# Linear ReLU attention on one core: loads in five runs of two octets and one of one, in place of two of three, two of two and one of one

## The chip, the core and the metric

The kernel runs on one core of a Trainium2 chip. The core has a matrix engine (PE, with its weight loads shown as PEld), a vector engine (DVE), a scalar engine (ACT), a general engine (POOL) and a synchronising engine (SP), and sixteen transfer (DMA) engines that are shared by all queues of the core. The metric is the time of one execution on the device in microseconds; the number compared is the median over several executions.

## The reference

```
Q, K, V: (8, 12, 512, 64) float32
Q_feat = maximum(0, Q)
K_feat = maximum(0, K)
KV          = einsum('bhkd,bhkv->bhdv', K_feat, V)
K_sum       = sum(K_feat, axis=2)
numerator   = einsum('bhqd,bhdv->bhqv', Q_feat, KV)
denominator = einsum('bhqd,bhd->bhq', Q_feat, K_sum)
return numerator / (denominator[..., None] + 1e-10)
```

There are 96 independent heads (8 x 12), each of 512 rows of 64 values. 37.75 MB are read and 12.58 MB are written.

## The kernel before

**Tiling.** Eight heads make an octet; there are `NO` = 12 octets, numbered 0 to 11. Of each input an octet is 128 partitions x 2048 values: 1 MB of float32 in memory, and 512 KB of bfloat16 once loaded, because the loads from POOL's queue convert while they copy. Octet 0 is special: its K and V are loaded unconverted by SP's and ACT's queues into `k8` and `v8`, and only its Q comes over POOL's queue.

**Rings.** K, V and Q of octets 1 to 11 go to the rings `k_all`, `v_all` and `q_all` with `RING` = 6 places; octet o lies at place (o - 1) mod 6. So octets 1 to 6 can be loaded at once, and octet 7 needs the place of octet 1.

**Runs.** `RUNS` lists how many neighbouring octets one load carries. For each run `load_octets(o, n)` issues three transfers on POOL's queue, in the order K, V, Q: `load_kv(Kr, ...)` and `load_kv(Vr, ...)` at line 106 and `load_q` at line 114 (line 111 when the run has one octet). A transfer's consumers wait until the whole transfer has landed, so the first octet of a run is not usable before the last one of that run.

**The plan.** POOL's transfers are issued in the fixed order of the list `plan`. It holds the loads of `RUNS` and, between and behind them, the stores of octets 0 to 9 (line 149); the stores of octets 10 and 11 are issued by SP (line 279). `pump(done)` runs through the plan after each octet. It issues a load once the places it overwrites have been read, and a store once its result is ready; nothing overtakes the head of the list:

```
last = o + n - 1 - RING
while done < last - HEAD + 1:          # HEAD = 4
    plan.append(("store", done, done))
...
if kind == "load" and o + n - 1 - RING <= done:
```

With the runs before, POOL's order is: Q of octet 0; octets 1 to 3; octets 4 to 6; octets 7 and 8; store 0; octets 9 and 10; store 1; octet 11; stores 2 to 9. Everything up to octet 6 is issued by the first call, `pump(0)`.

**Slots.** In the program as built, POOL's transfers take eight completion semaphores in turn. A transfer that is eight places behind another in POOL's order is issued only after that other one has landed, and POOL stands still for it.

**The octet loop.** For octet o, in program order: `kvs(o)` sums K-features times V over all rows on PE (line 196) and ACT copies the sums out of PSUM (line 205); `prep(2o+2)` masks the first half of K (DVE line 180) and V (DVE line 182) of octet o + 1, and `prep_v` does the other V mask (ACT line 187); `backs(o-1)` transposes the previous octet's result back (PE line 265), and DVE multiplies by the reciprocal denominator into `o_sb` (line 271), which is then stored; `denom(o)` (PE line 247; DVE lines 250, 255, 259); `out_t(o)` (PE line 237, ACT line 239); `prep(2o+3)` for the second half (DVE lines 180, 182, 189); `qt(o+1)` transposes Q of octet o + 1 (PE line 215, ACT line 220); `pump(o+1)`. So K and V of octet o + 1 are first needed early in the pass of octet o, and its Q at the end of that pass. Every engine takes its instructions in this order.

**Result tiles.** `o_sb` has seven buffers, two of which first hold `k8` and `v8`. The result of octet 9 goes to the buffer of octet 2, and so waits for store 2 to land.

Of the kernel before, what the change touches and what calls it, by code (L numbers as in the profile page):

```python
# [10 lines left out]
def kernel(  # L11
# [73 lines left out]
    q_sb, k_sb, v_sb = {}, {}, {}  # L85

    RING = DELAY + 1
    RUNS = (3, 3, 2, 2, 1)
    k_all = consts.tile([P, RING, RQ, D], bf16, name="k_all")
    v_all = consts.tile([P, RING, RQ, D], bf16, name="v_all")  # L90
    q_all = consts.tile([P, RING + 1, U, 2 * D], bf16, name="q_all")
# [38 lines left out]
    plan, o, done = [], 1, 0  # L130
    for n in RUNS:
        last = o + n - 1 - RING
# [231 lines left out]
```

## Time and profile before

| | |
|---|---|
| time, median of 3 | 127.46 us (126.89 to 127.71) |
| profiled execution, its own time | 128.06 us |
| its span in the profile | 126.1 us |
| mean granted PE clock | 0.91 |
| PE, DVE, ACT busy | 67%, 63%, 64% of the span |
| POOL's transfer queue (q0) | 28.31 MB in SBUF bytes, 90.2% of sixteen engines' span |

The span is what the profiler covers; the time around it (start and end of the execution) is the difference of 1.96 us. Busy shares are means over the whole span, and the first third of this kernel looks quite different from the rest. DMA rates are counted in SBUF bytes: a converting load reads twice what it writes, so it shows about half the rate of a store. All landing times below are an issue's start plus its time to landing.

### The profile page before, as it was taken

Reading aid. Unit: us, or ns where it says so; the run is one execution under the profiler, and the core shown is the slowest. Engines: PE = TensorE matmul, PEld = TensorE weight load, DVE = VectorE, ACT = ScalarE, POOL = GpSimd, SP = SyncE. Lnnn points to the kernel's source line nnn. Section 1 sums busy time; section 2 is a strip of 40 time slices with the busy share of each in tenths; the row PEclk is TensorE's granted clock in tenths of the full one; section 3 lists DMA queues with packets and bytes.
Section 4 is the critical chain, followed back from the end, with each engine's and each line's share of the span. In section 5 each row is a group of like instructions: output and inputs, shape, how many; then the busy total and the mean of one; then the engine's idle time right before and its main releaser. Section 6 shows DMA issues by size and latency. Waiting matters only on the chain.

```text
span 126.1 us, 3357 instructions
## 1 busy us (share of the span) xinstructions
PE 84.3 (67%) x1451; PEld 75.3 (60%) x1451; DVE 79.6 (63%) x175; ACT 80.4 (64%) x110; POOL 17.7 (14%) x32
## 2 busy tenths in 40 slices
PE   0005951000399898988989898998989899898600
PEld 0005940000399687878978787897878788796500
DVE  2709530067003979969696987969697896928510
ACT  0008840063065989899898989989898998975000
POOL 6920000000000070002604110110220010100000
PEclk9999985555558999999999999999999999999996
DMA  3999999999999999999999999999999999999762
GB/s 81 387 318 213 218 212 217 214 213 216 216 213 213 221 209 214 220 209 216 216 213 231 365 213 210 216 216 326 265 216 304 411 431 421 421 421 416 301 249 94
DMA packets 6638, 32.71 MB, mean 259 GB/s; under 512 B 480, under 2 KB 480, under 8 KB 4832
## 3 DMA queue, kind: packets, MB, share of 16 engines
q0 software_dynamic: 6048, 28.31, 90.2%
q1 hardware_dynamic: 432, 3.15, 6.3%
q10 hardware_dynamic: 144, 1.05, 2.1%
q8 instruction: 11, 0.18, 0.5%
q14 instruction: 3, 0.02, 0.0%
HBM read 37.75 MB, written 12.58 MB: 399 GB/s over the span
## 4 chain that ended last, share of the span: by engine, by line
DVE 40%; PE 25%; DMA 24%; issue 3%; POOL 2%; DVEq 1%; ACT 1%; ACTq 1%; POOLq 0%
DMA q_all<-in_Q_dram 24%; DVE o_sb L271 20%; PE ps_kv L196 12%; PE ps_bk L265 11%; DVE kf L180 5%; DVE den L255 3%; DVE vo_all L189 3%; DVE vo_all L182 3%; DVE rec L259 3%; DVE own L250 3%; PE ps_qt L215 1%; DVEq L359 1%; ACT ot_sb L239 1%; ACTq L359 1%; POOL v_all L106 1%
## 5 line engine op out<-in xcount | busy, mean ns | idle before, releaser
L271 DVE TENSOR_TENSOR o_sb<-ps_bk,rec 128x1024 f32<-128x1024 f32 x24 | 28.3, 1219 | 22.6 <-PE ps_bk L265 22.6
L215 PE MATMUL ps_qt<-ident,q_all 128*128 128x128 bf16 x192 | 14.3, 234 | 25.3 <-DMA q_all<-in_Q_dram 25.3
L196 PE MATMUL ps_kv<-vo_all,kf 64*128 64x132 bf16 x768 | 28.9, 230 | 1.2
L215 PEld LDWEIGHTS <-q_all 128*128 128x128 bf16 x192 | 13.0, 106 | 26.0 <-DMA q_all<-in_Q_dram 25.7
L196 PEld LDWEIGHTS <-kf 64*128 64x128 bf16 x768 | 25.4, 100 | 3.9 <-issue 2.9
L239 ACT COPY ot_sb<-ps_ot 128x1024 f32<-128x1024 f32 x24 | 24.1, 1013 | 4.3 <-PE ps_ot L237 3.6
L220 ACT ACTIVATE qt<-ps_qt 128x1024 bf16<-128x1024 bf16 x24 | 23.3, 1028 | 5.3 <-PE ps_qt L215 5.3
L265 PE MATMUL ps_bk<-ident,ot_sb 128*128 128x128 f32 x192 | 23.6, 276 | 0.7 <-ACT ot_sb L239 0.7
L205 ACT CAST kvd<-ps_kv 64x260 bf16<-64x260 f32 x48 | 18.0, 374 | 7.7 <-PE ps_kv L196 6.8
L265 PEld LDWEIGHTS ps_bk<-ident,ot_sb 128*128 128x128 f32 x192 | 20.7, 141 | 2.2 <-ACT ot_sb L239 0.9
L180 DVE TENSOR_SCALAR kf<-k_all,mask_k 128x1024 bf16<-128x1024 bf16 x44 | 18.4, 459 | 2.0 <-DMA k_all<-in_K_dram 2.0
L187 ACT ACTIVATE vo_all<-v_all,mask_v 128x1024 bf16<-128x1024 bf16 x11 | 12.7, 1154 | 9.4 <-DMA v_all<-in_V_dram 9.1
L237 PE MATMUL ps_ot<-qt,kvd 128*128 128x256 bf16 x96 | 14.7, 278 | 5.8 <-DVE o_sb L271 5.5
L182 DVE TENSOR_SCALAR vo_all<-v_all,mask_v 128x1024 bf16<-128x1024 bf16 x22 | 10.8, 492 | 7.3 <-DMA v_all<-in_V_dram 7.3
L237 PEld LDWEIGHTS <-kvd 128*128 128x128 bf16 x96 | 9.4, 99 | 9.3 <-issue 7.4
L106 POOL DMA_DIRECT2D k_all<-in_K_dram x5 | 3.6, 719 | 53.1 <-DVE kf L180 53.1
L149 POOL DMA_DIRECT2D out_dram<-o_sb x10 | 5.5, 547 | 32.7 <-DVE o_sb L271 15.3
L247 PE MATMUL ps_den<-kvd,qt 128*128 128x16 bf16 x192 | 7.0, 179 | 1.7 <-ACT kvd L205 1.7
L247 PEld LDWEIGHTS <-qt 128*128 128x128 bf16 x192 | 6.8, 96 | 1.9 <-issue 1.6
L187 ACT ACT_TABLE_LOAD x1 | 1.3, 1283 | 9.8 <-DMA v_first<-in_V_dram 9.8
L255 DVE TENSOR_REDUCE den<-own 128x32 f32<-128x256 f32 x12 | 5.0, 420 | 0.4
L189 DVE TENSOR_SCALAR vo_all<-v_all,mask_v 128x1024 bf16<-128x1024 bf16 x11 | 5.3, 480 | 0.0
(24 smaller groups left out, 31.4 us busy)
## 6 DMA issues: line engine op xcount, KB each, us to landing
out_dram<-o_sb POOLq DMA_DIRECT2D x10, 1024.0 KB, 21.3
k_all<-in_K_dram POOLq DMA_DIRECT2D x2, 1536.0 KB, 26.0
v_all<-in_V_dram POOLq DMA_DIRECT2D x2, 1536.0 KB, 33.0
q_all<-in_Q_dram POOLq DMA_DIRECT2D x2, 1536.0 KB, 39.5
k_all<-in_K_dram POOLq DMA_DIRECT2D x2, 1024.0 KB, 17.6
v_all<-in_V_dram POOLq DMA_DIRECT2D x2, 1024.0 KB, 21.5
q_all<-in_Q_dram POOLq DMA_DIRECT2D x2, 1024.0 KB, 25.7
out_dram<-o_sb SPq DMA_DIRECT2D x2, 1024.0 KB, 5.3
```

Of the source, the lines that this page charges most:

```text
L180: nc.vector.tensor_scalar(kf[g][:, :, s, :], k_sb[g], scalar1=0.0, scalar2=mask_k[:, s:s + 1], op0=Alu.max, op1=Alu.mult)
L182: nc.vector.tensor_scalar(vo[g % NB][:, :, 0, 2:D + 2], v_sb[g], scalar1=mask_v[:, 0:1], scalar2=None, op0=Alu.mult)
L187: nc.scalar.activation(vo[g % NB][:, :, 1, 2:D + 2], v_sb[g], Act.Copy, scale=mask_v[:, 1:2])
L196: nc.tensor.matmul(ps_kv[:, half, 0:2 * (D + 2)].rearrange("p (t d) -> p t d", t=2), kf[g][rows, r, :, :].rearrange("p s d -> p (s d)"), v ...
L205: nc.scalar.copy(kvd[o % NK][64 * c:64 * c + 64, s::2, c * D1:c * D1 + D1].rearrange("p (g t) d -> p g t d", t=2), ps_kv[64 * s:64 * s + 6 ...
L215: nc.tensor.transpose(ps[:, u, :], q_sb[o][:, i * (U // 2) + u, :], ident)
L220: nc.scalar.activation(qt_sb[o % NZ][:, i * (U // 2):(i + 1) * (U // 2)], transp(o, i), Act.Relu)
L237: nc.tensor.matmul(ps[:, i], kvd[o % NK][:, h, 1:2 * D + 1], q[:, :, h, :], start=True, stop=True, skip_group_check=True)
L239: nc.scalar.copy(ot[o][:, :, 4 * j:4 * j + 4], ps.rearrange("p h u c -> p u h c"))
L247: nc.tensor.matmul(ps[:, u], qt_sb[o % NZ][:, u, :], kvd[o % NK][:, :, 0:2 * D1:2 * D1 - 1], start=True, stop=True, skip_group_check=True)
L265: nc.tensor.transpose(ps[:, 2 * v:2 * v + 2].rearrange("p c d -> p (c d)"), ot[o][:, 8 * j + v].rearrange("p h c -> p (h c)"), ident32)
L271: nc.vector.tensor_tensor(o_sb[:, rs], ps, rec[o][:, rs].unsqueeze(2).to_broadcast([P, 16, D]), op=Alu.mult)
```

## The change

The list of runs is altered and nothing else. Octets 1 to 6 are loaded as 2 + 2 + 2 in place of 3 + 3; the runs of octets 7 to 11 stay 2, 2 and 1. With the same conditions in `pump`, all loads up to octet 6 still stand in the first call, now nine transfers in place of six, and POOL's list has three transfers more. The orders on PE, DVE, ACT and SP are the same in both programs. Because POOL's list is longer at its head, the eighth and ninth load (V and Q of octets 5 and 6) now take semaphore slots that were used before: V waits until Q of octet 0 has landed, and Q until K of octets 1 and 2 has.

```
     RING = DELAY + 1
-    RUNS = (3, 3, 2, 2, 1)
+    RUNS = (2, 2, 2, 2, 2, 1)
```

## The prediction

> **What bounds the kernel now.** First the head of the page and its slices (40 slices of 3.15 us).
>
> ```profile
> span 126.1 us, 3357 instructions
> PE   0005951000399898988989898998989899898600
> PEclk9999985555558999999999999999999999999996
> DMA  3999999999999999999999999999999999999762
> ```
>
> There are two stories in these rows. PE works a little, stands still in slices 7 to 9, and from slice 11 works at 80 to 90% until near the end. The transfer engines are busy from slice 1 to slice 36 without a gap. So I ask the chain of waits what ends last, and then the transfers what they would allow.
>
> ```profile
> 3.99 29.66 DMA q_all<-in_Q_dram
> 33.70 1.89 PE ps_qt L215 x16
> ...
> 40.03 2.36 DVE o_sb L271 x2
> ...
> 105.36 2.36 DVE o_sb L271 x2
> ...
> 119.29 1.13 DVEq L359
> ```
>
> The chain starts with one transfer, Q of octets 1 to 3; PE needs it for octet 1 and starts at 33.70. Behind that stands a loop of DVE and PE with no transfer in it: nine passes from 40.03 to 105.36, 7.26 us each. The last store is issued at 119.29 + 1.13 = 120.42. Read alone, the chain says that whatever octet 1 gains in landing, the end gains.
>
> The second limit is the stream of POOL's transfers; its tail is seen in fine windows. Columns: window, length, busy time of PE, PEld, DVE, ACT and POOL (instructions), granted clock, transfer engines' busy share, GB/s.
>
> ```profile
> 118.00:118.50 0.50, 0.50 (x7) 0.50 (x6) 0.44 (x1) 0.00 (x0) 0.00 (x0) 1.00 0.86 360
> 118.50:119.00 0.50, 0.40 (x4) 0.16 (x2) 0.50 (x1) 0.00 (x0) 0.00 (x0) 1.00 0.51 213
> ...
> 119.50:120.00 0.50, 0.00 (x0) 0.00 (x0) 0.50 (x1) 0.00 (x0) 0.00 (x0) 1.00 0.23 98
> 120.00:120.50 0.50, 0.00 (x0) 0.00 (x0) 0.42 (x1) 0.00 (x0) 0.00 (x0) 1.00 0.04 16
> 118.30:120.50 2.20, 0.60 (x6) 0.36 (x4) 2.12 (x2) 0.00 (x0) 0.00 (x0) 1.00 0.32 134
> 120.50:121.20 0.70, 0.00 (x0) 0.00 (x0) 0.00 (x0) 0.00 (x0) 0.00 (x0) 1.00 0.00 0
> 121.20:124.10 2.90, 0.00 (x0) 0.00 (x0) 0.00 (x0) 0.00 (x0) 0.00 (x0) 0.96 0.88 359
> 124.10:126.10 2.00, 0.00 (x0) 0.00 (x0) 0.00 (x0) 0.00 (x0) 0.00 (x0) 0.50 0.02 8
> ```
>
> Until 118.3 nearly all sixteen engines work. Then they run dry one after another, the last at about 120.5: the stores of octets 0 to 10 are through. Store 11, issued at 120.42, moves bytes from 121.2 to 124.1, and 2.0 us later the span ends. The whole idle time of the transfer engines is this tail, and that is all that an earlier computation can fill.
>
> **The change: when octet 1 lands.** Issue times come from POOL's timeline, landing times from the transfers' rows, for V of 1 to 3, K of 4 to 6 and Q of 4 to 6.
>
> ```profile
> 3.21 0.78 POOL L106 DMA_DIRECT2D v_all<-in_V_dram  x1
> 4.76 0.77 POOL L106 DMA_DIRECT2D k_all<-in_K_dram  x1
> 6.30 0.77 POOL L114 DMA_DIRECT2D q_all<-in_Q_dram  x1
> ...
> v_all<-in_V_dram POOLq DMA_DIRECT2D x1, 1536.0 KB, 23.1
> k_all<-in_K_dram POOLq DMA_DIRECT2D x1, 1536.0 KB, 36.3
> q_all<-in_Q_dram POOLq DMA_DIRECT2D x1, 1536.0 KB, 49.4
> ```
>
> V of 1 to 3 lands at 3.21 + 23.1 = 26.31, K of 4 to 6 at 41.06, Q of 4 to 6 at 55.70. The queue works in order, so I count octet-tiles of 512 KB behind Q of octet 0. V of 1 to 3 ends with tile 6 (K, K, K, V, V, V); after the change tile 6 ends Q of octets 1 and 2 (K, K, V, V, Q, Q). So octet 1 is complete at 26.31 in place of 33.70: 7.39 us earlier. Tile 12 ends Q of 3 and 4: 41.06. Tile 18 ends Q of 5 and 6: 55.70, as before. A tile takes (55.70 - 26.31) / 12 = 2.45 us; hence V of 3 and 4 (tile 10) at 36.1.
>
> **Three more transfers.** Their issue is 0.77 us each on POOL, which in the whole prologue does nothing else that anyone waits for; its issues run far ahead of the stream (Q of 4 to 6 is issued 49.4 us before it lands), so this costs nothing. The ninth transfer waits for its slot until Q of octet 0 has landed, the tenth until K of 1 and 2 has (tile 2, under 18 us): POOL stands still until then with seven or eight transfers still queued. Without that cover every us of POOL's delay would be a us of dry transfer engines. What a transfer itself costs the stream is seen from the single-octet loads.
>
> ```profile
> 66.34 0.62 POOL L106 DMA_DIRECT2D k_all<-in_K_dram  x1 [4.12 <-DVE kf L180]
> 67.36 0.78 POOL L106 DMA_DIRECT2D v_all<-in_V_dram  x1 [0.41 <-issue]
> ...
> k_all<-in_K_dram POOLq DMA_DIRECT2D x1, 512.0 KB, 26.6
> v_all<-in_V_dram POOLq DMA_DIRECT2D x1, 512.0 KB, 28.1
> ```
>
> K of octet 11 lands at 92.94 and V at 95.46: 2.52 us for one tile as a transfer of its own, against 2.45 us inside transfers of three. The cost of a cut is between 0 and about 0.1 us ((2.52 - 2.45) x 3 / 2); three cuts are 0 to 0.3 us. I take 0, since the last tile of the stream's first part has the same bytes ahead of it.
>
> The Trainium skill speaks against the change: the page "DMA: Bandwidth & Descriptors", section "Anatomy of one DMA — SWDGE (gpsimd) path", gives a transfer about 2.0 us plus its bytes over 436 GB/s, and so favours large ones. If the 2.0 us stood in the stream, an estimate from that page is 6 us for three transfers; the same section puts most of it into the completion, which does not hold up what is queued behind, and the 2.52 us above agree with that.
>
> **What becomes of 7.39 us.** The loop runs 7.39 us earlier until a transfer is late for it. The rows of need (before), V and Q of octet 3, V and Q of octet 9:
>
> ```profile
> 45.83 0.70 DVE L182 TENSOR_SCALAR vo_all<-v_all,mask_v 128x1024 bf16<-128x1024 bf16 x1
> 50.13 1.06 PE L215 MATMUL ps_qt<-ident,q_all 128*128 128x128 bf16 x16
> ...
> 89.32 0.48 DVE L182 TENSOR_SCALAR vo_all<-v_all,mask_v 128x1024 bf16<-128x1024 bf16 x1
> 93.69 1.06 PE L215 MATMUL ps_qt<-ident,q_all 128*128 128x128 bf16 x16
> ...
> 60.11 0.83 POOL L106 DMA_DIRECT2D v_all<-in_V_dram  x1 [0.33 <-issue]
> 60.93 0.72 POOL L114 DMA_DIRECT2D q_all<-in_Q_dram  x1
> v_all<-in_V_dram POOLq DMA_DIRECT2D x1, 1024.0 KB, 23.1
> q_all<-in_Q_dram POOLq DMA_DIRECT2D x1, 1024.0 KB, 27.1
> 73.23 0.59 POOL L149 DMA_DIRECT2D out_dram<-o_sb  x1 [1.70 <-DMA out_dram<-o_sb]
> out_dram<-o_sb POOLq DMA_DIRECT2D x1, 1024.0 KB, 28.0
> ```
>
> Octet 3: V wanted at 45.83 - 7.39 = 38.44, there at 36.1; Q wanted at 42.74, there at 41.06. No wait. Each further pair costs the loop 14.52 us and the stream 6 x 2.45 = 14.7 us, so octets 5 and 7 also hold with about 1.3 us to spare. Store 0 then puts a store between octets 8 and 9, at the same place of the stream as before. Octet 9: V lands at 60.11 + 23.1 = 83.21, wanted at 81.93: DVE stands 1.28 us, and behind it the write of octet 7's result. Q lands at 88.03, wanted at 87.58: 0.45 us. The lead is then 5.66 us. Octet 9's result needs store 2's buffer: that lands at 73.23 + 28.0 = 101.23, wanted at 105.36 - 5.66 = 99.70: 1.53 us. The lead at the end is 4.13 us, and the last store is issued at 116.3.
>
> **The end.** Nothing of the stream itself has moved: its bytes, order and rate are as before, and stores 2 to 9 are queued behind octet 11's load in both. What moves is store 11, whose bytes now follow store 10's without a gap. Its work is 2.90 x 0.88 = 2.55 us on each engine.
> - Late bound: the engine that ran dry last, 120.5, does its share after that: 123.05, plus 2.0 = 125.05.
> - Early bound: the work left after 118.3 (2.20 x 0.32 = 0.70 us) spread evenly: 118.3 + 0.70 + 2.55 + 2.0 = 123.55.
>
> Each engine has its own share of a transfer, so I stay near the late one. But its 2.0 us hold a straggler: the last row's 0.02 x 16 x 2.00 = 0.64 us is one engine still at work past 124.1. Without it the late bound is 124.4, which I take. Sum: 126.1 - 124.4 = **1.7 us** less; the lead of 4.13 us needs only 120.42 + 0.8 - 120.5 = 0.7 us to give this on the last engine. By the profiled execution's own 128.06 that is 126.4; it stood 0.6 us above the median, so against 127.46 it is **125.8 us**, 1.3% faster.
>
> **The rivals.**
> 1. *The clock takes the lead back, and nothing is to be measured.* The granted clock is halved in slices 6 to 11.
>
> ```profile
> 14.66:18.08 3.42, 1.76 (x52) 1.64 (x47) 0.54 (x6) 1.91 (x5) 0.00 (x0) 1.00 1.07 214
> 18.08:21.50 3.42, 1.18 (x7) 0.52 (x4) 0.88 (x2) 0.00 (x0) 0.00 (x0) 0.50 1.07 216
> 35.15:38.56 3.41, 3.41 (x61) 3.21 (x60) 0.00 (x0) 1.56 (x2) 0.00 (x0) 0.50 1.07 217
> ```
>
> A window with PE half busy (1.76 of 3.42 us) was followed by half the clock, and after work from 33.70 to 38.56 it returned: 4.86 us at half speed, 2.43 us lost. The new waits at octet 9 could do this again. One such fall alone leaves a lead of 5.66 - 2.43 = 3.23 us, and the wait for store 2 is gone (wanted at 102.1, there at 101.2): the forecast stands. Two leave 0.8 us, just enough for the late bound: 125.05, so 126.4; three leave none: 127.5. Against it: each wait is under 1.8 us and PE works around it. (The Trainium skill, "TensorE: Matmul & The Clock Gate", Part 1, lets the clock fall only after an idle window of some 3.4 us; by that rule these waits cost nothing, but the first row above differs from it.)
> 2. *All of the 7.39 us arrive*: 120.1 us. The chain supports it, the transfer engines' share of 0.9 and more in every slice denies it.
> 3. *Slower: every added transfer holds up the queue.* Place: the head of the stream, from which all later tiles are late by the same. Price c per transfer: the end moves by 3c - 1.7 us; from c = 0.6 us there is no gain, from c = 1.0 us it is slower by 1%. At 2 us, near the one-octet interval itself, 127.46 - 1.7 + 6 = 131.8. For it only the untested start, where converting and plain loads mix; against it the 2.52 us.
> 4. *It doesn't do what it says*: if the completion of a two-octet transfer came no earlier than that of three, PE would start at 33.7 as now: 127.5.
>
> **How the numbers follow.** A measurement of this kernel tells about 1% (1.27 us) from no change. Chances: forecast 0.72, of which 0.12 within 1% since the late bound of 125.05 is a gain of only 1.05 us; rival 1 0.12; rival 2 0.06; rival 3 0.08; rival 4 0.02. Faster 0.60 + 0.06 = 0.66, same 0.12 + 0.12 + 0.02 = 0.26, slower 0.08. The range: the bounds of the end give 124.9 (123.55) to 126.4 (125.05); the upper side takes in most of rival 1: 124.8 to 127.1.
>
> **What would show it.** Right: the first transpose of octet 1 at 26.3; DVE waiting for V of octet 9 about 1.3 us and for store 2 about 1.5 us; the last store issued near 116 to 117; no idle window of the transfer engines between 118 and 122; no wait for V or Q of octets 3 to 8. Wrong: Q of 5 and 6 landing later than 56; a gap in the transfer engines' share around 10 to 20 us; half the clock behind 80 us; or a span below 123.5.

## The result and the profile after

The changed kernel takes 126.41 us (median of 6 executions, 125.76 to 126.75) against 127.91 us for the kernel before beside it (126.89 to 128.43): ratio 0.9874, 95% interval 0.9837 to 0.9912. A second comparison gave 126.15 against 127.78 us, ratio 0.987, interval 0.9829 to 0.9912. So it is 1.3% faster; 125.8 us (a ratio of 0.987 to its reference of 127.46) had been forecast. The profiled execution took 125.76 us with a span of 123.8 us; the spans of the other five are 124.1 to 124.5.

Head of the page and slices, kernel after:

```profile
span 123.8 us, 3360 instructions
PE   0004943059989898998989899895499898997100
PEclk9999998555999999999999999999869999999975
DMA  3999999999999999999999999999999999999992
```

PE's long standstill is shorter (it works again from slice 8), and the transfer engines are now busy to slice 38 of 40: the ragged tail of 7, 6, 2 is gone. There is one new mark: PE at 5 and 4 tenths in slices 27 and 28, and a short fall of the clock in slices 28 and 29.

The chain of waits, kernel after (start, length, what):

```profile
3.89 22.35 DMA q_all<-in_Q_dram
...
26.29 1.89 PE ps_qt L215 x16
...
53.34 35.19 DMA q_all<-in_Q_dram
...
88.57 1.73 PE ps_qt L215 x16
...
115.44 1.13 DVEq L359
```

Octet 1's Q is there at 26.24 (33.65 before). But the chain has a second transfer in it now, Q of octets 9 and 10, which PE gets at 88.57: the loop has run so far ahead that the stream is late for it. The last store is issued at 116.57 (120.42 before), 3.85 us earlier. Of these the span shows 2.3 us in this pair of profiles, and the medians of the times 1.5 us.

The tail in windows, kernel after (columns as in the prediction):

```profile
118.00:118.50 0.50, 0.00 (x0) 0.00 (x0) 0.00 (x0) 0.00 (x0) 0.00 (x0) 1.00 1.13 475
...
120.00:120.50 0.50, 0.00 (x0) 0.00 (x0) 0.00 (x0) 0.00 (x0) 0.00 (x0) 0.50 1.01 426
120.50:121.00 0.50, 0.00 (x0) 0.00 (x0) 0.00 (x0) 0.00 (x0) 0.00 (x0) 0.50 0.66 279
121.00:121.50 0.50, 0.00 (x0) 0.00 (x0) 0.00 (x0) 0.00 (x0) 0.00 (x0) 0.50 0.54 229
121.50:122.00 0.50, 0.00 (x0) 0.00 (x0) 0.00 (x0) 0.00 (x0) 0.00 (x0) 0.50 0.50 213
122.00:122.50 0.50, 0.00 (x0) 0.00 (x0) 0.00 (x0) 0.00 (x0) 0.00 (x0) 0.50 0.16 66
122.50:123.00 0.50, 0.00 (x0) 0.00 (x0) 0.00 (x0) 0.00 (x0) 0.00 (x0) 0.50 0.00 0
```

Every engine of the core has finished before 118, and still the transfer engines work at full share to 120.5; then they run dry one after another until 122.5, with the same raggedness as the first dry-out before (118.3 to 120.5). The idle piece before store 11 is closed.

What the loop met on its way, kernel after, DVE in order of time, then PE's wait for Q of octet 9 and its clock around that:

```profile
32.43 2.36 DVE L271 TENSOR_TENSOR o_sb<-ps_bk,rec 128x1024 f32<-128x1024 f32 x2 [7.23 <-PE ps_bk L265]
...
83.57 0.49 DVE L182 TENSOR_SCALAR vo_all<-v_all,mask_v 128x1024 bf16<-128x1024 bf16 x1 [1.77 <-DMA v_all<-in_V_dram]
83.98 2.35 DVE L271 TENSOR_TENSOR o_sb<-ps_bk,rec 128x1024 f32<-128x1024 f32 x2
...
94.25 2.36 DVE L271 TENSOR_TENSOR o_sb<-ps_bk,rec 128x1024 f32<-128x1024 f32 x2 [4.07 <-PE ps_bk L265]
101.51 2.36 DVE L271 TENSOR_TENSOR o_sb<-ps_bk,rec 128x1024 f32<-128x1024 f32 x2 [1.04 <-PE ps_bk L265]
...
88.57 1.73 PE L215 MATMUL ps_qt<-ident,q_all 128*128 128x128 bf16 x16 [1.59 <-DMA q_all<-in_Q_dram]
...
85.44:88.85 3.41, 1.28 (x13) 0.78 (x12) 3.34 (x8) 2.03 (x2) 0.00 (x0) 0.99 1.03 338
88.85:92.27 3.42, 3.42 (x55) 3.23 (x54) 1.33 (x4) 1.94 (x2) 1.37 (x2) 0.51 1.05 240
```

The same two results, of octets 7 and 8, in the kernel before:

```profile
90.85 2.35 DVE L271 TENSOR_TENSOR o_sb<-ps_bk,rec 128x1024 f32<-128x1024 f32 x2 [1.05 <-PE ps_bk L265]
...
98.11 2.36 DVE L271 TENSOR_TENSOR o_sb<-ps_bk,rec 128x1024 f32<-128x1024 f32 x2 [1.05 <-PE ps_bk L265]
```

The lead is 40.03 - 32.43 = 7.60 us at the first result. At octet 9 DVE waits 1.77 us for V. This wait takes the place of the 1.05 us that DVE waits for PE there in the kernel before, so the lead falls only to 90.85 - 83.98 = 6.87 us. Then PE waits 1.59 us for Q; it is busy for only 1.28 of a 3.41 us window, its clock is halved in the next, and DVE's next result waits 4.07 us for PE. The lead is now 98.11 - 94.25 = 3.86 us, and it stays so (105.36 - 101.51 = 3.85) up to the end.

### The profile page after: what moved, and what is told of

The parts are those of the page before. It is cut to its first block, busy times and chain, and to the rows that moved or that the text cites. A ratio compares the mean times of both kernels' runs of the same rounds, so it can differ in the third digit from the quotient of the medians.

```text
span 123.8 us, 3360 instructions
## 1 busy us (share of the span) xinstructions
PE 85.9 (69%) x1451; PEld 76.9 (62%) x1451; DVE 79.9 (65%) x175; ACT 80.5 (65%) x110; POOL 19.6 (16%) x35
## 3 DMA queue, kind: packets, MB, share of 16 engines
q10 hardware_dynamic: 144, 1.05, 2.3%
## 4 chain that ended last, share of the span: by engine, by line
DMA 46%; DVE 21%; PE 19%; POOL 2%; issue 2%; DVEq 1%; ACT 1%; ACTq 1%; POOLq 0%
DMA q_all<-in_Q_dram 46%; DVE o_sb L271 11%; PE ps_kv L196 9%; PE ps_bk L265 7%; PE ps_qt L215 3%; DVE kf L180 2%; DVE den L255 2%; DVE vo_all L182 2%; DVE vo_all L189 2%; DVE rec L259 1%; DVE own L250 1%; POOL v_all L106 1%; DVEq L359 1%; ACT ot_sb L239 1%; ACTq L359 1%
## 5 line engine op out<-in xcount | busy, mean ns | idle before, releaser
L196 PE MATMUL ps_kv<-vo_all,kf 64*128 64x132 bf16 x768 | 30.1, 237 | 1.1
L196 PEld LDWEIGHTS <-kf 64*128 64x128 bf16 x768 | 26.7, 103 | 3.8 <-issue 2.9
L215 PE MATMUL ps_qt<-ident,q_all 128*128 128x128 bf16 x192 | 15.0, 241 | 19.2 <-DMA q_all<-in_Q_dram 19.2
L215 PEld LDWEIGHTS <-q_all 128*128 128x128 bf16 x192 | 13.5, 109 | 20.0 <-DMA q_all<-in_Q_dram 19.8
L237 PE MATMUL ps_ot<-qt,kvd 128*128 128x256 bf16 x96 | 14.2, 271 | 6.5 <-DVE o_sb L271 6.3
L182 DVE TENSOR_SCALAR vo_all<-v_all,mask_v 128x1024 bf16<-128x1024 bf16 x22 | 10.9, 493 | 5.1 <-DMA v_all<-in_V_dram 5.1
L106 POOL DMA_DIRECT2D k_all<-in_K_dram x6 | 4.2, 698 | 36.0 <-DVE kf L180 31.5
L187 ACT ACT_TABLE_LOAD x1 | 1.3, 1283 | 10.1 <-DMA v_first<-in_V_dram 10.1
L106 POOL DMA_DIRECT2D v_all<-in_V_dram x6 | 4.4, 730 | 9.4 <-DVE vo_all L189 4.9
L180 DVE TENSOR_SCALAR kf<-k_first,mask_k 128x1024 bf16<-128x1024 f32 x4 | 2.8, 748 | 3.9 <-DMA k_first<-in_K_dram 3.9
```

What stands on the lines that cost most here:

```text
L180: nc.vector.tensor_scalar(kf[g][:, :, s, :], k_sb[g], scalar1=0.0, scalar2=mask_k[:, s:s + 1], op0=Alu.max, op1=Alu.mult)
L182: nc.vector.tensor_scalar(vo[g % NB][:, :, 0, 2:D + 2], v_sb[g], scalar1=mask_v[:, 0:1], scalar2=None, op0=Alu.mult)
L187: nc.scalar.activation(vo[g % NB][:, :, 1, 2:D + 2], v_sb[g], Act.Copy, scale=mask_v[:, 1:2])
L196: nc.tensor.matmul(ps_kv[:, half, 0:2 * (D + 2)].rearrange("p (t d) -> p t d", t=2), kf[g][rows, r, :, :].rearrange("p s d -> p (s d)"), v ...
L215: nc.tensor.transpose(ps[:, u, :], q_sb[o][:, i * (U // 2) + u, :], ident)
L237: nc.tensor.matmul(ps[:, i], kvd[o % NK][:, h, 1:2 * D + 1], q[:, :, h, :], start=True, stop=True, skip_group_check=True)
```

## Experiments

The theories: **A**, the end is set by the stream of transfers, and the gain is the idle piece of its tail; **B**, the end follows the chain from octet 1's landing to the last store, us by us; **C**, each further transfer costs the queue; **D**, the waits at octet 9 took the rest of the gain; **E**, POOL's queue makes some transfer engines lag at the end. Ratios are against the kernel before, run beside.

**1. Octet 1 still earlier** (on the changed kernel):

```
-    RUNS = (2, 2, 2, 2, 2, 1)
+    RUNS = (1, 2, 2, 1, 2, 2, 1)
```

> Runs of 1, 2, 2, 1, 2, 2, 1 octets: octet 1 arrives alone, at about 18.9 us in place of 26.3. Theory A (the end is set by the transfer stream, which has no gap left to close): PE starts 7.4 us earlier than in the changed kernel and the end does not move: span 123.8 to 124.5, time within 0.5 us of the changed kernel, 0.985 to 0.99 of the kernel before. Theory B (the chain from the landing of octet 1 to the last store sets the end): at least 2 us and up to 7 us faster than the changed kernel. Theory C (each further transfer costs the queue): a little slower than the changed kernel, by three times the price.

Measured: 126.75 us, ratio 0.9899 (0.9866 to 0.9933), so no faster than the changed kernel. PE did start earlier:

```profile
19.11 1.90 PE L215 MATMUL ps_qt<-ident,q_all 128*128 128x128 bf16 x16
...
33.72 1.89 PE L215 MATMUL ps_qt<-ident,q_all 128*128 128x128 bf16 x16 [1.37 <-DMA q_all<-in_Q_dram]
```

Octet 1's first transpose comes 7.2 us before that of the changed kernel (26.29), and 14.6 us before that of the kernel before, and none of the 7.2 us arrive. Most of them are lost one octet later: Q of octets 2 and 3 comes only at 33.7, so octet 2's transposes start 1.6 us before those of the changed kernel (35.28). The last store goes out at 115.88, 0.7 us earlier (116.57 there). So B falls in its plain form, but mostly because the stream takes the lead back on the way; of the end itself this run shows only that 0.7 us of lead bring nothing.

**2. Every octet by itself** (18 more load transfers than before):

```
-    RUNS = (2, 2, 2, 2, 2, 1)
+    RUNS = (1,) * 11
```

> All eleven runs of one octet: 33 load transfers in place of 18 in the changed kernel and 15 in the kernel before. Theory A: within 0.5 us of the changed kernel, and the interval between two landings stays 2.45 us per tile. Theory C: slower than the changed kernel by 15 times the price of a transfer: 1.5 us at 0.1 us, 30 us at 2 us.

Measured: 126.51 us, ratio 0.9885 (0.9814 to 0.9956), the changed kernel's time. POOL's timeline shows the stream's step: with eight slots, every issue waits for the landing eight places before it.

```profile
27.00 0.53 POOL L106 DMA_DIRECT2D v_all<-in_V_dram  x1 [1.90 <-DMA q_all<-in_Q_dram]
...
51.88 0.84 POOL L111 DMA_DIRECT2D q_all<-in_Q_dram  x1 [1.97 <-DMA k_all<-in_K_dram]
```

Between these rows there are ten steps: 24.88 / 10 = 2.49 us per tile, against 2.45 inside transfers of three. By the prediction's own sum a cut costs (2.49 - 2.45) x 3 / 2 = 0.06 us. Read from the end it is less: the spans, 124.4 to 124.8 us, lie some 0.4 us above those of the changed kernel, 0.03 us for each of 15 further transfers. So the three cuts of the change cost 0.1 to 0.2 us, and C falls at any price that could be measured here. DVE's waits for stores are the price of coming early:

```profile
DVE o_sb L271 <- DMA out_dram<-o_sb: 13.2, 3, 4.9
```

13.2 us of waiting for result buffers (three times, 4.9 us the longest) come on top of 10.1 us of waiting for V. The last store goes out at 117.03, 0.5 us later than in the changed kernel, and the time stays.

**3 and 4. Delay the last store** with idle work on DVE, on the changed kernel (3) and on the kernel before (4):

```
     idle(6, NO - 1)
+    for _ in range(9):
+        zero_kv(0)
     backs(NO - 1)
```

> The changed kernel with nine idle memsets (0.49 us each, 4.4 us) on DVE ahead of the last two result instructions; DVE stood still 1.9 us there, so the last store is issued some 2.5 us later, at about 119. Theory A: there is that much slack, since the transfer engines still have stores queued: the time moves by 0 to 0.5 us. Theory B: 2.5 us slower than the changed kernel.

> The kernel before with the same nine memsets. Theories A and B: its transfer engines are dry when the last store comes, so all of the delay arrives: 2.5 us slower than before, ratio 1.02. If it moves by less than 1 us, the tail of the kernel before was not set by its last store and theory A is wrong.

Measured: 127.85 us, ratio 0.9961 (0.9917 to 1.0005), on the changed kernel; 131.47 us, ratio 1.027 (1.0197 to 1.0343), on the kernel before. My sizing was off: a memset took 0.67 us with its gap, so in 3 the last store was issued 4.0 us later (120.53 against 116.57), not 2.5, and in 4 DVE's delay was 3.9 us. So 3 moved more than I had written, by 1.4 us of 4.0 by the medians and 1.1 by the ratios, and 4 by 3.5 us. At 120.53 the last store of 3 goes out when that of the kernel before does (120.42), and the time is again that of the kernel before within 0.4%. The slack is there but ends between 2.6 and 2.9 us. Hence the smaller pad:

**5 and 6. The same with six memsets**, and the changed kernel beside them.

> The changed kernel with six memsets ahead of the last two result instructions. In the trace of the nine-memset kernel one took 0.67 us with its gap, so six are 4.0 us, of which 1.9 us fill a standstill: the last store is issued 2.1 us later, near 118.6. Theory A: its bytes can move from 119.4 on, when nearly all transfer engines still have stores of their own to move; the time is within 0.6 us of the changed kernel run beside it. Theory B: 2.1 us slower.

> The kernel before with the same six memsets. Theories A and B: the whole 2.1 us arrives, ratio about 1.016.

> The changed kernel once more, to stand beside these two: ratio about 0.987. Theory A adds: the spans of the kernel before differ with the granted clock (its chain sets the end), those of the changed kernel do not.

Measured: 126.28 us with the pad against 126.15 us without, ratios 0.9873 (0.9832 to 0.9914) and 0.987 (0.9829 to 0.9912). The last store is issued 116.47 + 2.29 = 118.76 in place of 116.59, and the time does not move. The transfer engines of the padded kernel in windows of 1 us:

```profile
118.00:119.00 1.00, 0.00 (x0) 0.00 (x0) 0.75 (x1) 0.00 (x0) 0.00 (x0) 1.00 0.59 246
119.00:120.00 1.00, 0.00 (x0) 0.00 (x0) 0.00 (x0) 0.00 (x0) 0.00 (x0) 0.78 0.64 270
120.00:121.00 1.00, 0.00 (x0) 0.00 (x0) 0.00 (x0) 0.00 (x0) 0.00 (x0) 0.50 1.00 418
```

Some engines stand idle from 118 to 120 (shares 0.59 and 0.64). The trace's transfer records carry no engine's name, but they can be counted: three engines are still at work when store 11's bytes begin at 119.6, and three end it late, at 122.6 to 123.0, against 122.1 to 122.3 for the other thirteen. So the end is that of the engines that lag, and as far as a count can show it these have no gap. This is the "late bound" of the prediction at work.

On the kernel before, the same pad cost only 0.84% (0.47 to 1.20%), 1.07 us in place of the 2.1 expected. SP's last wait tells why (engine, line, waited for: total, times, longest); first the kernel before, then the padded one:

```profile
SPq L359 <- DMA out_dram<-o_sb: 4.0, 1, 4.0
...
SPq L361 <- DMA out_dram<-o_sb: 3.1, 1, 3.1
```

Store 11 itself is 0.9 us shorter in the padded kernel. The transfer records suggest a cause: in the kernel before, 8 KB of the instruction queue were moved at 122.56 us, in the middle of store 11, and one transfer engine ended 0.8 us after the last of the other fifteen; with the pad the 8 KB came at 112.61, and all sixteen ended within 0.2 us. The other traces in which store 11 ran alone say the same. In experiments 7, 8 and 10 the 8 KB fell into it, one engine was 0.8 us late and SP's last wait was 4.0 us; in 3 and 4 they came earlier, no engine was late, and the wait was 2.9 and 3.1 us. So 1.9 us of delay (the padded DVE needs 7.32 us from octet 10's result to octet 11's, 5.44 without) less 0.9 is the 1.0 us measured. That this one transfer made the straggler is read from seven traces, not tried by itself; its own record lasts 0.31 us, and why the engine is 0.8 us late stays open.

**7 and 8. Take the stream out of the way**: stores of octets 2 to 9 write half their rows, on the kernel before (7) and the changed one (8).

```
+ half = slice(0, RQ // 2 if o >= 2 else RQ)
- nc.gpsimd.dma_start(out=Or[o].rearrange(...), in_=ready[o], ...)
+ nc.gpsimd.dma_start(out=Or[o].rearrange(...)[:, half], in_=ready[o][:, half], ...)
```

> The kernel before, with the stores of octets 2 to 9 writing only half of each row (the other half of those results is left out): the stream becomes 8 x 1.2 = 10 us shorter behind octet 11's load. Theory A: the kernel before is set by its chain and its last store, so it gains nothing or little, 0 to 0.7 us. Theory B: the same.

> The changed kernel with the same half stores (half of the results of octets 2 to 9 is left out). Theory A: with the stream out of the way the whole remaining lead of the chain (3.9 us in the profile) arrives: 3.5 to 4.5 us below the half-store kernel with the runs before, span about 122. Theory B': the lead was lost elsewhere and the stream has no part in it: the difference stays at 1.5 to 2.3 us.

Measured: 127.70 us, ratio 0.9962 (0.9929 to 0.9995), with the runs before; 123.59 us, ratio 0.9649 (0.9603 to 0.9695), with the changed runs. Span and transfer slices of 7, then of 8:

```profile
span 126.1 us, 3357 instructions
DMA  4999999999999999999999999999999994402552
...
span 121.6 us, 3360 instructions
DMA  3999999999999999999999999999999999914462
```

Both tails are now thin, so in both the chain ends last. With the runs before, 8 x 0.5 MB fewer bytes gain 0.4%: next to nothing waited for them. With the changed runs they gain 2.3% (0.9649 against 0.9874). The two kernels with half stores lie 4.1 us apart (127.70 - 123.59), and their last stores, at 120.46 and 115.91 us, 4.55: now nearly the whole lead arrives, although DVE still waits for V of octet 9 in 8 (1.66 us). The change of runs is worth 1.5 us with the full stores and 4.1 us with half of them: the stream keeps the difference.

**9. Octet 9 as a run of its own, ahead of store 0** (on the changed kernel):

```
-    RUNS = (2, 2, 2, 2, 2, 1)
+    RUNS = (2, 2, 2, 2, 1, 1, 1)
```

> Runs of 2, 2, 2, 2, 1, 1, 1: octet 9 comes as a transfer of its own and ahead of store 0, so its V lands near 75 us, well before it is wanted. Theory A: the wait for V of octet 9 and the fall of the clock behind it vanish, DVE then waits some 3 us for store 2's buffer, and the end stays where it is in the changed kernel, within 0.5 us. Theory D (the waits at octet 9 ate the lead and so the gain): 2 to 4 us faster than the changed kernel.

Measured: 126.65 us, ratio 0.9884 (0.9836 to 0.9933): the changed kernel's time again. DVE no longer waits for octet 9's V, and waits for the buffers of stores 1 and 2:

```profile
90.49 2.35 DVE L271 TENSOR_TENSOR o_sb<-ps_bk,rec 128x1024 f32<-128x1024 f32 x2 [1.31 <-DMA out_dram<-o_sb]
101.36 2.35 DVE L271 TENSOR_TENSOR o_sb<-ps_bk,rec 128x1024 f32<-128x1024 f32 x2 [4.67 <-DMA out_dram<-o_sb]
```

One wait of the stream's takes the place of another. The clock fell behind this wait too, which I had not expected. The last store goes out at 118.47, 1.9 us later than in the changed kernel, and the time stays, as A has it. For D alone this is no clean test, since the lead at the end is smaller here and not larger; D falls because 2 us less of lead do not move the end (this run and experiment 5), and because in experiment 8 the lead that is left behind those waits arrives.

**10. Stores 8 and 9 on SP's queue as well** (on the changed kernel):

```
-    plan += [("store", i, i) for i in range(done, NO - 2)]
+    plan += [("store", i, i) for i in range(done, NO - 4)]
...
-        if o >= NO - 2:
+        if o >= NO - 4:
```

> The changed kernel with the stores of octets 8 and 9 on SP's queue as well, so four stores there. Theory A: the same bytes on the same sixteen engines, so the same end within 0.5 us. Theory E (POOL's queue makes some engines lag, by about 2 us at the end): up to 1.5 us faster.

Measured: 127.22 us, ratio 0.9929 (0.9883 to 0.9975), with executions from 126.26 to 128.21. Not faster, so E has no support; whether it is a little slower is inconclusive. Nor is E refuted: the profile kept is of the longest of these executions, where DVE waits 5.17 us for a result buffer, the clock falls behind that, and the last store goes out at 120.44 to engines that are dry again. Why some engines run dry 2 us before others stays open.

All together: the changed kernel and experiments 1, 2, 5 and 9 issue their last store between 115.9 and 118.8 us in their profiles, and their times are 126.2 to 126.8 us. Experiment 3 issues it at 120.5 and takes 127.9 us, like the kernel before (120.4). None of the variants with whole stores beats the changed kernel.

## Why the prediction was right

**The landing times: right.** Counting octet-tiles of 512 KB in the stream gave 26.31 for octet 1 and 55.70 for Q of octets 5 and 6. Octet 1's Q was in use at 26.29; the tenth transfer of the kernel after was held by its slot until 16.25 and landed at 16.25 + 39.5 = 55.75:

```profile
16.25 0.71 POOL L114 DMA_DIRECT2D q_all<-in_Q_dram  x1 [4.10 <-DMA k_all<-in_K_dram]
...
q_all<-in_Q_dram POOLq DMA_DIRECT2D x1, 1024.0 KB, 39.5
```

POOL's new standstills were far from being felt: the bytes of this transfer had their turn only at 55.75 - 2 x 2.45 = 50.85, some 34 us after its issue.

**Three more transfers at nothing: right.** Experiment 2 made the cost 0.03 to 0.06 us each, inside the 0 to 0.1 us bounded before. The 2.0 us that the Trainium skill's page "DMA: Bandwidth & Descriptors" (section "Anatomy of one DMA — SWDGE (gpsimd) path") gives per transfer did not stand in this queue, which always had the next transfer behind.

**Where 7.39 us go: right in place, off in its parts.** No wait appeared for V or Q of octets 3 to 8, and the first late transfer was V of octet 9: 1.77 us where 1.28 had been worked out. The lead was 7.60, not 7.39, since PE's clock came back 4.5 us after its start and not 4.9. V and Q of octets 9 and 10 landed at 83.51 and 88.54, 0.3 and 0.5 us later than in the kernel before; the three cuts explain 0.1 to 0.2 of that, the rest is open. None of the three waits cost what was put down for it. V cost 0.73 us of lead and not 1.28, since it covers the 1.05 us that DVE waits for PE there anyhow. Q was late by 1.59 us and not 0.45, and with the fall of the clock behind it cost 3.01 us. The wait for store 2's buffer (1.53 us) disappeared. So one fall came, as rival 1 had described it, with a lead of 3.23 us and the forecast standing. Half the clock behind 80 us was also on the prediction's list of signs of being wrong; it came, and by rival 1's own argument it refutes nothing. That 3.85 us of lead were left where 4.13 had been forecast is luck, since the parts are different ones. The rule of "TensorE: Matmul & The Clock Gate" in the Trainium skill (Part 1), a fall only after an idle window, does not describe these windows (1.28 of 3.41 us busy, and 1.76 of 3.42 before).

**The end: right, with one term taken without a reason.** 124.4 us had been taken between 123.55 and 125.05; the profiles show 123.8 and 124.4, and all twelve executions lie between 123.8 and 124.5. The transfer records decide between the two bounds: the last byte moves at 122.61 and 123.15 us in the two profiles of the changed kernel and at 123.03 in experiment 5, where the late bound says 123.05 and the early one 121.55. So the engine that lags most sets the end, and idle gaps on the others cost nothing. That some 0.6 us of the old tail were a straggler was right too (experiment 6: 0.9 us). But that it would be missing after the change was assumed and not argued, and that it is missing is luck: in the changed kernel the 8 KB move at 118.87, when every engine still has other bytes to move, and the last four engines end within 0.14 us. That little of the lead is needed was right in kind: 2.2 us of it can be thrown away for 0.13 us. The gain is the idle tail and not the lead. This is shown from both sides: by a last store that goes out 1.9 or 2.2 us later without loss and 0.7 us earlier without gain (experiments 9, 5 and 1), and by less stream with more gain (7 and 8).

## What to carry to other kernels

When a chain starts with a transfer and the transfer engines are busy throughout, ask first how much idle time the engines have left: here that, and not the earlier start, was what cutting the first load could bring. Count the stream in units of equal bytes; the position of a tile in the queue gives its landing time after a regrouping, without a model. To see which limit ends last, delay the end of one and thin out the other, one at a time: here 2.2 us of delay cost next to nothing and fewer stored bytes nearly tripled the gain.

## What the runs showed of the hardware

In the kernel before, bound by its chain, the span goes with the PE clock: over 55 executions the median span is 126.6 us where the mean granted clock was 0.90 (15 executions), 126.1 at 0.91 (24) and 125.4 at 0.92 (16). The changed kernel's twelve show hardly any of it: 124.3, 124.3 and 124.05 us at 0.91, 0.92 and 0.93. That fits an end set by the transfers; it also means that part of what looked like noise before went with the clock. What puts an execution at 0.90 or at 0.92 is not shown.

PE's clock was halved after windows of 3.4 us in which it was busy for 51% (kernel before, 1.76 of 3.42 us) and 38% (kernel after, 1.28 of 3.41 us), and stayed whole after the one ahead of the latter, with 78% (2.67 of 3.42 us). Windows of this length fit the times at which the clock changed: 18.08 and 38.56 us before, six of them apart, and 88.85 and 92.27 after, one apart. What share of busy time decides, somewhere between 51% and 78% by these rows, was not tried.

In all four traces in which 8 KB of the instruction queue were moved inside store 11 while it ran alone, one of sixteen transfer engines ended 0.8 us behind the rest; in the three in which they came earlier, none did. In the kernel before, that engine set the end.
